# One decoder layer on one core: order of the last up-projection taps and of the residual row scaling

## The chip, the cores and the metric

The kernel runs on one core of one Trainium2 chip. The metric is the device time of an execution in microseconds; the time before is 735.07 us, the median of 3 runs (734.85 to 735.47). One further execution was profiled, and every duration below comes from it.

## The reference

One decoder layer with 512 tokens and a model width of 1024, in float32. Two causal attention branches on the same modulated input are gated, merged and projected; then a residual sum with a layer norm; then a gated MLP with a causal depthwise convolution of width 3 between the up-projection and the SiLU gate; then a second residual sum with a layer norm:

```python
x = _layer_norm(DEEPNORM_ALPHA * x + (1.0 + gt1) * attn_out, ln1_g, ln1_b)
u2 = x * (1.0 + sc2) + sh2
h = _causal_depthwise_conv(u2 @ w_up, conv_w, conv_b)
h_gate, h_val = jnp.split(h, 2, axis=-1)
ffn_out = (jax.nn.silu(h_gate) * h_val) @ w_down
x = _layer_norm(DEEPNORM_ALPHA * x + (1.0 + gt2) * ffn_out, ln2_g, ln2_b)
```

`w_up` is 1024 x 5632 and `w_down` 2816 x 1024. The change touches the stage that computes `h` and the start of the stage behind it.

## The kernel before, in words

**Products.** Every float32 operand is split into a high half (rounded to fp32r) and a low half (the rest), and each product is three matmuls: high x high, high x low, low x high (`mm3`, lines 152 to 154; `product`, lines 1148 to 1150). For weights, `split_proc` makes the halves `wh` on ACT (line 217) and `wl` on DVE (line 94).

**The up-projection** is a loop over 44 tiles n = 0 to 43, each of 128 columns (`for n in range(2 * FT)`). A tile is 24 matmuls over 512 tokens into one PSUM bank `ps`. ACT reads the bank with an Identity that applies the last tap and the bias (line 1201), DVE adds the two other taps (lines 1202 and 1203). Only then is the bank free again. After an odd tile ACT computes SiLU of the gate (line 1209) and DVE multiplies (line 1210). After every fourth tile `blocks` prepares the operands of the down-projection, and `early_products` does 18 of its matmuls ahead (line 1148 to 1150). From tile 7 on, six of the eight banks hold sums of the down-projection (`yz`), so the up-projection has two banks, and tile n+2 takes the bank of tile n.

**Behind the loop** `phase(Z, zi, ...)` multiplies pairs of down-projection weights (`zi`, split by `split_cols`) into two new banks, `Z`. These are the two banks of tiles 42 and 43.

**Residual rows.** `x1[i]` holds the normalized rows of the first sub-layer (tiles named `xn`, four row blocks of two halves). They need scale and bias of the layer norm, times alpha, before the second residual sum. `o_x1(i, e)` does that for a half: one multiplication (line 975) and one addition (line 976) on DVE. The first call also loads the four half rows `lnr` by broadcasts on SP (`ln_row`, line 913) and lets ACT scale them (lines 916 and 919). It is called at the even tiles 6 to 20.

**Loads.** `weights(i, ahead)` asks for the weights of item i and those some items ahead: up-projection weights (`in_wup`), parts of `w_down` (`in_wdp`), columns of the modulation matrix (`in_wa`), whose products are summed on DVE by `mod_sum` (line 240). All go through five buffers `raw` by SP's queue. Two parts of `w_down` are added during the transfer by an accumulating load from POOL (line 181).

**What sets the order.** SP's loads stand in program order. The instructions of the other engines are put in order by the framework's scheduler, engine by engine, by its own estimates; a wait is placed only where data or a buffer asks for it. `tc.issue_after(x)` is an edge for this scheduler: the instruction does not stand ahead of x.

Of the kernel before, what the change touches and what calls it, by code (L numbers as in the profile page):

```python
# [11 lines left out]
AF = mybir.ActivationFunctionType  # L12
ALU = mybir.AluOpType
# [9 lines left out]
FT = DFF // P  # L23
# [28 lines left out]
def layer_kernel(ctx: ExitStack, tc: tile.TileContext, out, xT, x, c8, wa0, wa1, bcol, w1, wct, wv, bf,  # L52
# [3 lines left out]
    V, S, G, PE = nc.vector, nc.scalar, nc.gpsimd, nc.tensor  # L56
# [14 lines left out]
    cnt, state = [0], {"load": 0, "proc": 0}  # L71

    def nm(s):
        cnt[0] += 1
        return f"{s}_{cnt[0]}"

    def bank():
        return pp.tile([P, 512], F32, name=nm("ps"), tag="ps")
# [5 lines left out]
    def const(shape, dt, s):  # L84
        return cons.tile(shape, dt, name=s, tag=s)
# [7 lines left out]
    def lo_of(o, i, hi):  # L93
        state["read"] = V.tensor_tensor(o, i, fl(hi), ALU.subtract)  # L94
        return state["read"]
# [33 lines left out]
    g = G.tensor_copy(crow[0:KT], c8s)  # L129
# [18 lines left out]
    def z(dt, s, shape=(P, 512)):  # L148
        return zp.tile(list(shape), dt, name=nm(s), tag="z", bufs=NZ)
# [7 lines left out]
    reads, held, pins, convs = [], [], {}, []  # L157
# [56 lines left out]
    def split_proc(r, cols=1024):  # L214
        h = stg.tile([P, 1024], F32R, name=nm("wh"), tag="wh", bufs=WBUFS)
        l = stg.tile([P, 1024], F32R, name=nm("wl"), tag="wl", bufs=WBUFS)
        state["hi"] = S.activation(h[:, 0:cols], r[:, 0:cols], AF.Copy)  # L217
        lo_of(l[:, 0:cols], r[:, 0:cols], h[:, 0:cols])
        return h, l
# [477 lines left out]

    def split_cols(cols):
        def f(r):
            return split_proc(r, cols)  # L700
        return f

    stream, sums = [], []
# [206 lines left out]
    def ln_row(n):  # L910
        t = [z(F32, "lnr") for _ in range(2)]
        for e in range(2):
            nc.sync.dma_start(t[e], lnrow[n : n + 1, e * 512 : (e + 1) * 512].broadcast_to([P, 512]))
        if n % 2 == 0:
            for e in range(2):
                S.activation(t[e], t[e], AF.Copy, scale=-0.5 * ALPHA)
        else:
            for e in range(2):
                S.activation(t[e], t[e], AF.Copy, scale=ALPHA)
        return t  # L920

    cw = const([P, 2 * FT, 4], F32, "cw")
    nc.sync.dma_start(cw, cwb)
    x1 = []
    lnr = []
# [46 lines left out]
    def o_x1(i, e):  # L972
        if not lnr:
            lnr.extend([ln_row(0), ln_row(1)])
        V.tensor_tensor(x1[i][e], x1[i][e], lnr[0][e], ALU.mult)
        V.tensor_tensor(x1[i][e], x1[i][e], lnr[1][e], ALU.add)

    def raw_proc(r):
        return r
# [57 lines left out]
    for n in range(2 * FT):  # L1037
# [7 lines left out]
        if n in (23, 27):  # L1045
            t = t13[(23, 27).index(n)][:, 0:512]
# [11 lines left out]
    zi, vi, xi, cli, wi = [], [], [], [], []  # L1058
# [112 lines left out]
    for n in range(2 * FT):  # L1171
        if n < NSPLIT:
            h, l = items[wui[n]][4]
            ps = bks[n]
            up_mm(ps, h, l, slice(256, 512))
        else:
            ps = bank()
            h, l = weights(wui[n], min(LOADS - 1, wui[min(n + 2, 2 * FT - 1)] - wui[n]))
            up_mm(ps, h, l, slice(0, 512))
            if n % 2 == 0 and 6 <= n < 22:  # L1180
                o_x1((n - 6) // 4, n // 2 % 2 == 0)
            if n >= 7 and n % 4 == 3:
                early_products((n - 7) // 4)
            if n in (10, 28):
                weights(wai[n], 0)
            if n in (10, 30):
                rows = gate_rows(1 + n // 30, G)
                next(rows)
            if n in (11, 32):
                next(rows)  # L1190
        if n == 24:
            for i in range(2):
                lnr2.append(lnp.tile([P, D], F32, name=f"ln2_{i}", tag=f"ln2_{i}"))
                nc.sync.dma_start(lnr2[i], lnrow[2 + i : 3 + i, :].broadcast_to([P, D]))
        if n == 28:
            S.activation(lnr2[0], lnr2[0], AF.Copy, scale=-0.5)
        if n in (30, 32):
            S.dma_start(out[(n - 30) * 64 : (n - 30) * 64 + P, :], lnr2[1])
        t = z(F32, "cv")
        hc.append(t)  # L1200
        S.activation(t, ps, AF.Identity, bias=cw[:, n, 3:4], scale=cw[:, n, 2:3])  # L1201
        V.scalar_tensor_tensor(t[:, 1:], ps[:, 0:511], cw[:, n, 1:2], t[:, 1:], ALU.mult, ALU.add)  # L1202
        convs.append(V.scalar_tensor_tensor(t[:, 2:], ps[:, 0:510], cw[:, n, 0:1], t[:, 2:], ALU.mult, ALU.add))  # L1203
        if n > 3:
            next(work, None)
        if n % 2 == 1:
            g, v = hc
            hc = []
            S.activation(g, g, AF.Silu)  # L1209
            V.tensor_tensor(g, g, v, ALU.mult)  # L1210
            hs.append(g)
            if n % 4 == 3:
                work = blocks(*hs)
                hs = []
                if n < 2 * FT - 1:
                    next(work)
# [9 lines left out]
    r = x1  # L1226
# [92 lines left out]
    lnr = lnr2  # L1319
# [13 lines left out]
    for n, k in enumerate(wi):  # L1333
        w = weights(k)
        for a, p in enumerate(range(2 * n, min(FP - LATE, 2 * n + 2))):
            t = ops[p][3]
# [10 lines left out]
    for i in range(2):  # L1347
        pieces = [(1, 0, 512)] if i == 0 else [(1, 0, 256), (1, 256, 512)]
        for n, (e, c0, c1) in enumerate(pieces):
            ps = bank()[:, 0 : c1 - c0] if i else W1[0]  # L1350
            for m in range(2 * n):
                PE.matmul(ps, idr, rest[:, m * 256 : m * 256 + 256], start=m == 0, stop=False)
            for q in range(LATE):
                t = ops[FP - LATE + q][3]
# [75 lines left out]
```

## Time and profile before

| | |
|---|---|
| median of 3 runs | 735.07 us (734.85 to 735.47) |
| the profiled execution | 734.44 us, its span 732.6 us |
| PE busy | 723.3 us, 99% of the span |
| DVE busy | 600.7 us, 82% |
| ACT busy | 391.6 us, 53% |
| POOL busy | 87.9 us, 12% |
| granted clock of PE | 0.998 |

PE is the matmul engine, PEld its weight loads, DVE, ACT and POOL the vector, scalar and general engines, SP the engine that issues loads; q1 is SP's DMA queue, q0 POOL's, q10 ACT's. In a row of the timeline stand start and duration in us, the engine, the line, the operation, out<-in by the program's names, and in brackets the idle time before it and what ended it. A row of waits reads: who waited, for whom, us in total, times, the longest. Durations of single instructions overlap a little at their ends, so the distance between two starts tells what an instruction costs its engine. A line can be a helper's, and then the tile names tell which call it is.

### The profile page before, as it was taken

What the parts mean: (1) busy time and instruction counts of PE and PEld (TensorE: products, weight loads), DVE (VectorE), ACT (ScalarE), POOL (GpSimd) and SP (SyncE); (2) the same over time, 40 slices, a digit from 0 to 9 for tenths busy, and PEclk for the clock granted to TensorE, in tenths of its full rate; (3) what the DMA queues carried; (4) which work ended last, traced back from release to release, by engine and by line L of the source; (5) the groups of instructions that cost most, each with busy time, mean ns of one, the idle gap of its engine ahead of it and who ended that gap; (6) DMA issues with size and microseconds to landing.
All of it is one profiled execution on the core that took longest, in us unless ns stands there. A gap on an engine that the chain in (4) does not pass through costs nothing.

```text
span 732.6 us, 9845 instructions
## 1 busy us (share of the span) xinstructions
PE 723.3 (99%) x3444; PEld 602.2 (82%) x3444; DVE 600.7 (82%) x1041; ACT 391.6 (53%) x684; POOL 87.9 (12%) x142
## 2 busy tenths in 40 slices
PE   8999999999999999999999999999999999999996
PEld 5878888888888888888889888888888888888885
DVE  7978799778898886873687999977887787679996
ACT  5576466686885754442056553454453444347550
POOL 1045224352010000000000001000011010000010
PEclk9999999999999999999999999999999999999999
DMA  9953535423332241632075677577799777656734
GB/s 357 404 207 126 174 116 198 148 88 115 118 116 103 71 171 59 221 130 86 1 259 146 209 248 245 166 247 229 206 339 254 211 239 208 200 161 226 223 86 95
DMA packets 45490, 131.96 MB, mean 180 GB/s; under 512 B 6168, under 2 KB 7200, under 8 KB 45440
## 3 DMA queue, kind: packets, MB, share of 16 engines
q1 hardware_dynamic: 38176, 112.61, 44.7%
q0 software_dynamic: 4224, 10.30, 7.0%
q10 hardware_dynamic: 3040, 8.42, 3.1%
q8 instruction: 27, 0.44, 0.2%
q14 instruction: 23, 0.19, 0.1%
HBM read 118.39 MB, written 12.85 MB: 179 GB/s over the span
## 4 chain that ended last, share of the span: by engine, by line
PE 97%; DMA 1%; DVE 1%; ACT 0%; issue 0%; DVEq 0%
PE ps L152 19%; PE ps L154 19%; PE ps L153 19%; PE ps L1148 5%; PE ps L1149 5%; PE ps L1150 5%; PE ps L369 5%; PE ps L613 3%; PE ps L595 2%; PE ps L521 2%; PE ps L523 2%; PE ps L522 2%; PE ps L939 2%; PE ps L940 2%; PE ps L941 2%; PE ps L547 1%
## 5 line engine op out<-in xcount | busy, mean ns | idle before, releaser
L217 ACT ACTIVATE wh<-raw 128x1024 fp32r<-128x1024 f32 (+1 forms) x105 | 109.1, 1041 | 106.2 <-PE ps L153 44.3
L94 DVE TENSOR_TENSOR wl<-raw,wh 128x1024 fp32r<-128x1024 f32 (+2 forms) x114 | 137.2, 1204 | 33.2 <-ACT wh L217 32.4
L152 PE MATMUL ps<-u2h,wh 128*128 128x512 f32 (+1 forms) x376 | 141.4, 376 | 0.0
L153 PE MATMUL ps<-u2l,wh 128*128 128x512 f32 (+1 forms) x376 | 141.2, 375 | 0.0
L154 PE MATMUL ps<-u2h,wl 128*128 128x512 f32 (+1 forms) x376 | 141.2, 375 | 0.0
L154 PEld LDWEIGHTS ps<-u2h,wl 128*128 128x128 f32 x376 | 70.8, 188 | 12.8
L152 PEld LDWEIGHTS ps<-u2h,wh 128*128 128x128 f32 x376 | 70.8, 188 | 12.8
L153 PEld LDWEIGHTS ps<-u2l,wh 128*128 128x128 f32 x376 | 70.8, 188 | 12.6
L152 PE MATMUL ps<-uh,wh 128*128 128x512 f32 x200 | 79.5, 398 | 0.0
L154 PE MATMUL ps<-uh,wl 128*128 128x512 f32 x200 | 78.3, 391 | 0.0
L153 PE MATMUL ps<-ul,wh 128*128 128x512 f32 x200 | 77.9, 390 | 0.0
L1201 ACT ACTIVATE cv<-ps,cw 128x512 f32<-128x512 f32 x44 | 34.0, 773 | 46.6 <-PE ps L154 40.2
L1202 DVE SCALAR_TENSOR_TENSOR cv<-ps,cw,cv 128x511 f32<-128x511 f32 x44 | 32.8, 744 | 22.6 <-ACT cv L1201 22.6
L154 PEld LDWEIGHTS ps<-uh,wl 128*128 128x128 f32 x200 | 37.5, 188 | 8.6 <-DVE wl L94 0.3
L153 PEld LDWEIGHTS ps<-ul,wh 128*128 128x128 f32 x200 | 37.6, 188 | 7.4
L152 PEld LDWEIGHTS ps<-uh,wh 128*128 128x128 f32 x200 | 37.5, 188 | 7.4
L240 DVE SCALAR_TENSOR_TENSOR raw<-raw,cbc 128x1024 f32<-128x1024 f32 x32 | 39.5, 1238 | 0.0
L575 POOL TENSOR_TENSOR pt<-pt,om 128x127 f32<-128x127 f32 (+3 forms) x32 | 38.6, 1218 | 1.4 <-DVE om L574 1.3
L181 POOL DMA_DIRECT2D raw<-in_wdp x10 | 8.8, 885 | 245.1 <-DMA raw<-in_wdp 229.2
L1203 DVE SCALAR_TENSOR_TENSOR cv<-ps,cw,cv 128x510 f32<-128x510 f32 x44 | 32.7, 743 | 0.4
L574 DVE TENSOR_TENSOR_SCAN om<-om,dg 128x127 f32<-128x127 f32 (+3 forms) x32 | 28.8, 960 | 3.8 <-ACT om L569 3.8
L1209 ACT ACTIVATE cv<-cv 128x512 f32<-128x512 f32 x22 | 13.9, 631 | 33.0 <-DVE cv L1203 33.0
(245 smaller groups left out, 1550.1 us busy)
## 6 DMA issues: line engine op xcount, KB each, us to landing
raw<-in_wup SPq DMA_DIRECT2D x44, 512.0 KB, 5.1
raw<-in_wa SPq DMA_DIRECT2D x32, 512.0 KB, 3.5
raw<-in_wct SPq DMA_DIRECT2D x25, 512.0 KB, 4.5
raw<-in_wdp SPq DMA_DIRECT2D x20, 512.0 KB, 5.2
wa<-in_wa SPq DMA_DIRECT2D x16, 512.0 KB, 8.7
raw<-in_wdp SPq DMA_DIRECT2D x22, 256.0 KB, 4.6
raw<-t SPq DMA_DIRECT2D x22, 256.0 KB, 4.1
raw<-in_wdp POOLq DMA_DIRECT2D x10, 512.0 KB, 7.3
```

Source lines behind the costliest of these rows:

```text
L94: state["read"] = V.tensor_tensor(o, i, fl(hi), ALU.subtract)
L152: PE.matmul(ps, wh, ah, start=first, stop=False)
L153: PE.matmul(ps, wh, al, start=False, stop=False)
L154: return PE.matmul(ps, wl, ah, start=False, stop=last)
L217: state["hi"] = S.activation(h[:, 0:cols], r[:, 0:cols], AF.Copy)
L240: state["read"] = V.scalar_tensor_tensor(wt[:, c], wt[:, c], 1.0, cbc[:, c] if by is None else by, ALU.mult, ALU.mult, accum_out=o)
L369: m = PE.matmul(grp[g], w, u, start=j == 0 and n == 0, stop=j == KT - 1 and n == 2)
L575: G.tensor_tensor(pt[b][:, s : e - 1], pt[b][:, s : e - 1], om[:, s + 1 : e], ALU.mult)
L1148: PE.matmul(ps, ah, bh, start=first, stop=False, skip_group_check=onto)
L1149: PE.matmul(ps, ah, bl, start=False, stop=False, skip_group_check=onto)
L1150: return PE.matmul(ps, al, bh, start=False, stop=last, skip_group_check=onto)
L1201: S.activation(t, ps, AF.Identity, bias=cw[:, n, 3:4], scale=cw[:, n, 2:3])
```

## The change

Line numbers of the changed kernel are 4 to 10 higher behind the first edit (the taps are lines 1206 to 1208 there, the scaling 980 and 981, SiLU of the last tile 1217).

- The split of Z's weights from the second pair on (`zi[2:]` is compared with the item number) is to stand behind SiLU of the last pair of tiles on ACT and behind the last tap on DVE, once that SiLU exists.
- That SiLU is to stand behind the Identity of tile 43.
- `o_x1` is called at tiles 8 to 22 instead of 6 to 20, in the same order of halves, and each call is to stand behind the last tap of the tile before.

```diff
     def split_cols(cols):
         def f(r):
-            return split_proc(r, cols)
+            with ExitStack() as order:
+                if "tap" in state and state["proc"] in zi[2:]:
+                    order.enter_context(tc.issue_after(state["tap"].ins))
+                    order.enter_context(tc.issue_after(convs[-1].ins))
+                return split_proc(r, cols)
         return f
...
     def o_x1(i, e):
         if not lnr:
             lnr.extend([ln_row(0), ln_row(1)])
-        V.tensor_tensor(x1[i][e], x1[i][e], lnr[0][e], ALU.mult)
-        V.tensor_tensor(x1[i][e], x1[i][e], lnr[1][e], ALU.add)
+        with tc.issue_after(convs[-1].ins):
+            V.tensor_tensor(x1[i][e], x1[i][e], lnr[0][e], ALU.mult)
+            V.tensor_tensor(x1[i][e], x1[i][e], lnr[1][e], ALU.add)
...
-            if n % 2 == 0 and 6 <= n < 22:
-                o_x1((n - 6) // 4, n // 2 % 2 == 0)
+            if n % 2 == 0 and 8 <= n < 24:
+                o_x1((n - 8) // 4, n // 2 % 2 == 1)
...
-        S.activation(t, ps, AF.Identity, bias=cw[:, n, 3:4], scale=cw[:, n, 2:3])
+        tap = S.activation(t, ps, AF.Identity, bias=cw[:, n, 3:4], scale=cw[:, n, 2:3])
...
-            S.activation(g, g, AF.Silu)
+            with ExitStack() as order:
+                if n == 2 * FT - 1:
+                    order.enter_context(tc.issue_after(tap.ins))
+                    state["tap"] = S.activation(g, g, AF.Silu)
+                else:
+                    S.activation(g, g, AF.Silu)
```

What the scheduler makes of it, at three places. First ACT at the end of the loop, before and now (`cv_6187` is tile 42, `cv_6243` tile 43, `wh_6316` the high half of Z's third item of weights, `wdh` parts of the last down-projection weights):

```order
L1201 ACTIVATE cv_6187<-ps_6151,cw 128x512
L1209 ACTIVATE cv_6187<-cv_6187 128x512
L217 ACTIVATE wh_6316<-raw_6265 128x1024
L1201 ACTIVATE cv_6243<-ps_6191,cw 128x512
L91 ACTIVATE wdh_6268<-raw_6157 128x512
```

```order
L1206 ACTIVATE cv_6187<-ps_6151,cw 128x512
L1206 ACTIVATE cv_6243<-ps_6191,cw 128x512
L1217 ACTIVATE cv_6187<-cv_6187 128x512
L91 ACTIVATE wdh_6268<-raw_6157 128x512
L217 ACTIVATE wh_6316<-raw_6265 128x1024
```

The split moved from ahead of tile 43's Identity to behind it and one more split. DVE there, before and now:

```order
L1203 SCALAR_TENSOR_TENSOR cv_6187<-ps_6151,cw,cv_6187 128x510
L94 TENSOR_TENSOR wl_6317<-raw_6265,wh_6316 128x1024
L1202 SCALAR_TENSOR_TENSOR cv_6243<-ps_6191,cw,cv_6243 128x511
L1203 SCALAR_TENSOR_TENSOR cv_6243<-ps_6191,cw,cv_6243 128x510
L94 TENSOR_TENSOR wdl_6269<-raw_6157,wdh_6268 128x512
```

```order
L1207 SCALAR_TENSOR_TENSOR cv_6243<-ps_6191,cw,cv_6243 128x511
L1208 SCALAR_TENSOR_TENSOR cv_6243<-ps_6191,cw,cv_6243 128x510
L94 TENSOR_TENSOR wdl_6269<-raw_6157,wdh_6268 128x512
L1220 TENSOR_TENSOR cv_6187<-cv_6187,cv_6243 128x512
L94 TENSOR_TENSOR wdl_6274<-raw_6192,wdh_6272 128x512
L94 TENSOR_TENSOR wl_6317<-raw_6265,wh_6316 128x1024
```

The low half `wl_6317` moved from ahead of tile 43's taps to behind them, a product and two half-wide splits. Second, SP's loads around tile 8, before and now (`raw_4307` before and `raw_4305` now are tile 10's weights):

```order
L174 DMA raw_4127<-in_wup 128x1024
L913 DMA lnr_4173<-in_lnrow 128x512
L913 DMA lnr_4174<-in_lnrow 128x512
L913 DMA lnr_4179<-in_lnrow 128x512
L913 DMA lnr_4180<-in_lnrow 128x512
L174 DMA raw_4192<-in_wa 128x1024
L174 DMA raw_4194<-in_wup 128x1024
L174 DMA raw_4261<-in_wdp 128x1024
L174 DMA raw_4264<-in_wdp 128x512
L174 DMA raw_4307<-in_wup 128x1024
```

```order
L174 DMA raw_4127<-in_wup 128x1024
L174 DMA raw_4178<-in_wa 128x1024
L174 DMA raw_4180<-in_wup 128x1024
L174 DMA raw_4247<-in_wdp 128x1024
L174 DMA raw_4250<-in_wdp 128x512
L917 DMA lnr_4280<-in_lnrow 128x512
L917 DMA lnr_4281<-in_lnrow 128x512
L917 DMA lnr_4286<-in_lnrow 128x512
L917 DMA lnr_4287<-in_lnrow 128x512
L174 DMA raw_4305<-in_wup 128x1024
```

The four loads of `lnr` moved behind four weight loads. Third, DVE from tile 8's first tap to tile 9's, before and now (`cv_4296` and `cv_4294` are tile 8, `cv_4350` and `cv_4348` tile 9; the rows of `raw` alone are sums of parts of `w_down`):

```order
L1202 SCALAR_TENSOR_TENSOR cv_4296<-ps_4260,cw,cv_4296 128x511
L94 TENSOR_TENSOR fo_4301<-cv_4058,fh_4300 128x256
L1203 SCALAR_TENSOR_TENSOR cv_4296<-ps_4260,cw,cv_4296 128x510
L94 TENSOR_TENSOR fo_4301<-cv_4187,fh_4300 128x256
L999 TENSOR_TENSOR raw_4309<-raw_4309 128x512
L94 TENSOR_TENSOR wdl_4319<-raw_4309,wdh_4317 128x512
L94 TENSOR_TENSOR wl_4379<-raw_4372,wh_4378 128x1024
L94 TENSOR_TENSOR wdl_4320<-raw_4309,wdh_4318 128x512
L975 TENSOR_TENSOR xn_3452<-xn_3452,lnr_4173 128x512
L646 SCALAR_TENSOR_TENSOR gcol<-modr,bcols 128x4
L1202 SCALAR_TENSOR_TENSOR cv_4350<-ps_4306,cw,cv_4350 128x511
```

```order
L94 TENSOR_TENSOR wl_4310<-raw_4305,wh_4309 128x1024
L1207 SCALAR_TENSOR_TENSOR cv_4294<-ps_4246,cw,cv_4294 128x511
...
L1003 TENSOR_TENSOR raw_4307<-raw_4307,raw_4247 128x512
L94 TENSOR_TENSOR wl_4377<-raw_4370,wh_4376 128x1024
L1004 TENSOR_TENSOR raw_4307<-raw_4307 128x512
L94 TENSOR_TENSOR wdl_4317<-raw_4307,wdh_4315 128x512
L240 SCALAR_TENSOR_TENSOR raw_4374,modr<-raw_4374,cbc 128x1024
L94 TENSOR_TENSOR wdl_4318<-raw_4307,wdh_4316 128x512
L94 TENSOR_TENSOR wl_4381<-raw_4372,wh_4380 128x1024
L1207 SCALAR_TENSOR_TENSOR cv_4348<-ps_4304,cw,cv_4348 128x511
```

The low half of tile 10's weights (`wl_4310`) now stands ahead of tile 8's first tap, and a mod sum (L240) and tile 12's split (`wl_4381`) ahead of tile 9's, where a multiplication of the row scaling and a small sum stood. The rows of PE are the same in number; around the early products a few of them change places, and one early product stands ahead of tile 11 now.

## The prediction

> **What bounds the kernel now.** I read the page first (busy shares, then the chain that ended last), then the waits of the matmul engine, then the stage of the up-projection in stretches of one period, and only then single instructions. The page:
>
> ```profile
> PE 723.3 (99%) x3444; PEld 602.2 (82%) x3444; DVE 600.7 (82%) x1041; ACT 391.6 (53%) x684; POOL 87.9 (12%) x142
> ...
> PE 97%; DMA 1%; DVE 1%; ACT 0%; issue 0%; DVEq 0%
> ```
>
> PE is busy for 723.3 of 732.6 us and holds 97% of the chain. 99% could still hide short waits, so here are all the waits of PE that the trace lists:
>
> ```profile
> PE ps L229 <- DVE warm L107: 1.2, 1, 1.2
> PE ps L229 <- DVE wa L240: 0.3, 1, 0.3
> PE ps L369 <- DVE uh L331: 0.3, 1, 0.3
> ```
>
> All three (L229 and L369) belong to the first stage, far ahead of the change. What is left of the 9.3 us without PE is the start and the tail after the last matmul. The periods of four up-projection tiles (columns: stretch, length, then busy time of PE, PEld, DVE, ACT, POOL):
>
> ```profile
> 401.93:427.77 25.84, 25.84 (x115) 21.40 (x114) 22.70 (x39) 14.93 (x26) 0.87 (x1) 1.00 0.67 216
> 427.77:453.61 25.84, 25.84 (x115) 21.40 (x114) 25.16 (x43) 13.06 (x22) 2.95 (x5) 1.00 0.79 252
> 453.61:479.45 25.84, 25.84 (x115) 21.40 (x114) 22.89 (x41) 10.98 (x19) 2.02 (x3) 1.00 0.64 191
> 479.45:505.29 25.84, 25.84 (x115) 21.40 (x114) 21.73 (x36) 11.87 (x20) 1.47 (x2) 1.00 0.74 227
> ```
>
> Every period lasts the same 25.84 us with PE busy through all of it at the full granted clock (the 1.00). DVE is nearly full in the second (25.16), where the row scaling sits, and PE does not notice. So neither edit can shorten these stretches: what a gain would be made of is a PE wait, and there must be one in reach.
>
> **Edit one, the taps of the last tile.** Busy time alone does not show it, the starts of the matmuls do:
>
> ```profile
> 662.37 0.39 PE L1148 MATMUL ps<-wh,hv 128*128 128x512 f32 x1
> 662.60 0.39 PE L1149 MATMUL ps<-wl,hv 128*128 128x512 f32 x1
> 663.10 0.47 PE L1148 MATMUL ps<-wh,hv 128*128 128x512 f32 x1
> ```
>
> The first two start 0.23 us apart, as matmuls of this form do elsewhere; the next gap is 0.50. The matmul at 663.10 is the first into the second bank of Z, and that bank is the last tile's, free only when both DVE taps have read it:
>
> ```profile
> 659.21 1.04 ACT L217 ACTIVATE wh<-raw 128x1024 fp32r<-128x1024 f32 x1
> 660.16 0.76 ACT L1201 ACTIVATE cv<-ps,cw 128x512 f32<-128x512 f32 x1
> ...
> 660.29 1.22 DVE L94 TENSOR_TENSOR wl<-raw,wh 128x1024 fp32r<-128x1024 f32 x1 [1.71 <-ACT wh L217]
> 661.43 0.74 DVE L1202 SCALAR_TENSOR_TENSOR cv<-ps,cw,cv 128x511 f32<-128x511 f32 x1
> 662.21 0.75 DVE L1203 SCALAR_TENSOR_TENSOR cv<-ps,cw,cv 128x510 f32<-128x510 f32 x1
> ...
> 666.36 0.39 PE L1149 MATMUL ps<-wl,hv 128*128 128x512 f32 x1
> ```
>
> The second tap ends at 662.96, and PE goes on 0.14 later. The split of the third pair of Z's weights stands ahead on both engines (ACT 659.21, DVE 660.29). The change puts it behind: the ACT tap can start at 659.21 instead of 660.16, the DVE taps at 660.29 or before instead of 661.43, and they end by 661.82. PE wants the bank at 662.60 + 0.23 = 662.83. The wait of 0.50 - 0.23 = **0.27 us** is gone. The price: the DVE half of that split now follows the two taps, one product and two half-splits. From a start at 660.29 that is 1.53 + 3 x 0.61 + 1.14, so it ends near 664.8. PE reads it at 666.36, or 666.1 without the wait: covered, with 1.3 us to spare.
>
> **Edit two, the row scaling.** Its instructions and loads, in the view of the tile lnr:
>
> ```profile
> L975 DVE TENSOR_TENSOR xn<-xn,lnr x8: 677/682/683, 421.6 to 459.0; 128x512 f32<-128x512 f32 x8
> L976 DVE TENSOR_TENSOR xn<-xn,lnr x8: 678/682/693, 422.9 to 459.7; 128x512 f32<-128x512 f32 x8
> L913 SPq DMA_DIRECT2D lnr<-in_lnrow x4: 376/400/432, 410.6 to 412.1; - x4
> ```
>
> The 16 operations (0.68 us each, about 11 us) stay 16. They ran from 421.6 to 459.7 and now run on to tile 22. Spreading them gains nothing, since PE never waited for DVE there. A period receives four of them: 4 x 0.61 = 2.4 us on top of 21.73 in the period that had none makes 24.2 of 25.84. At tiles 10, 14, 18 and 22 they stand ahead of and between the taps and delay these by at most 1.2 us. That the bank bears, for example at tile 10:
>
> ```profile
> 448.53 0.74 DVE L1203 SCALAR_TENSOR_TENSOR cv<-ps,cw,cv 128x510 f32<-128x510 f32 x1
> ...
> 453.61 0.39 PE L152 MATMUL ps<-u2h,wh 128*128 128x512 f32 x1
> ```
>
> Tile 10's taps end at 449.27, tile 12 takes the bank at 453.61: 4.3 us to spare. All this costs nothing.
>
> What is not free is that **the four loads of lnr move** behind four weight loads on SP, straight ahead of tile 10's weights. DMA traffic from 405 to 440 us, and the instructions that I use:
>
> ```profile
> q1 hardware_dynamic: 2160, 6.55, 56.3%
> q0 software_dynamic: 144, 0.52, 8.6%
> ...
> 423.00 0.38 SPq L174 DMA_DIRECT2D raw<-in_wup  x1
> ...
> 424.98 0.87 POOL L181 DMA_DIRECT2D raw<-in_wdp  x1 [29.72 <-DMA raw<-in_wdp]
> ...
> 425.37 1.21 DVE L240 SCALAR_TENSOR_TENSOR raw<-raw,cbc 128x1024 f32<-128x1024 f32 x1
> ...
> 426.51 0.74 DVE L1203 SCALAR_TENSOR_TENSOR cv<-ps,cw,cv 128x510 f32<-128x510 f32 x1
> ...
> 428.48 1.06 ACT L217 ACTIVATE wh<-raw 128x1024 fp32r<-128x1024 f32 x1 [0.58 <-DMA raw<-in_wup]
> ...
> 434.56 0.74 DVE L1202 SCALAR_TENSOR_TENSOR cv<-ps,cw,cv 128x511 f32<-128x511 f32 x1
> 435.22 0.41 DVE L94 TENSOR_TENSOR fo<-cv,fh 128x256 fp32r<-128x256 f32 x1
> 435.55 0.74 DVE L1203 SCALAR_TENSOR_TENSOR cv<-ps,cw,cv 128x510 f32<-128x510 f32 x1
> 436.21 0.42 DVE L94 TENSOR_TENSOR fo<-cv,fh 128x256 fp32r<-128x256 f32 x1
> 436.54 0.68 DVE L999 TENSOR_TENSOR raw<-raw 128x512 f32<-128x512 f32 x1
> 437.15 0.68 DVE L94 TENSOR_TENSOR wdl<-raw,wdh 128x512 fp32r<-128x512 f32 x1
> 437.75 1.22 DVE L94 TENSOR_TENSOR wl<-raw,wh 128x1024 fp32r<-128x1024 f32 x1
> 438.88 0.69 DVE L94 TENSOR_TENSOR wdl<-raw,wdh 128x512 fp32r<-128x512 f32 x1
> ...
> 438.42 0.39 PE L154 MATMUL ps<-u2h,wl 128*128 128x512 f32 x1
> ...
> 444.09 0.39 PE L152 MATMUL ps<-u2h,wh 128*128 128x512 f32 x1
> ```
>
> SP's queue (q1) moved 6.55 MB in 56.3% of 35 us, 0.33 MB per us of engine time. Tile 10's weights were asked for at 423.00 and landed about 428.5, when ACT split them. Call their new landing X. Four lnr loads are 1.05 MB, 3.2 us, now ahead of them: X = 431.7 at best. POOL's accumulating load (0.52 MB, 8.6% of 35 us = 3.0 us) shares the engines; it was beside this load before too, but now it meets the lnr loads as well. If all of it counts, X = 434.7. Below 431.7 nothing speaks for it, as the bytes ahead are certain. The nearest row, the old landing beside the same accumulate, lies by the low end; a third to a half of the accumulate is new, so I take **X = 432.9**.
>
> What hangs on X: in the new order ACT's split of tile 10 comes after the lnr scaling and ahead of tile 8's tap, DVE's split likewise, and the tap waits behind them. ACT 1.06 and DVE 1.14 put tile 8's first tap at X + 2.2. From there to the end of tile 9's second tap DVE now has: two taps 0.66 each and two half-splits 0.33 each, four 512-wide operations 0.61, two 1024-wide splits 1.13, the mod sum 1.14 (drawn forward from behind tile 9, with a split of tile 12), tile 9's taps 0.66 and 0.74 with 0.34 between. All are start-to-start distances of the rows above (the mod sum's is 425.37 to 426.51, the 0.34 is taken like the 0.33). Sum 9.56 us. The tap ends at X + 11.8, and PE can go on at X + 11.9. Tile 11 takes this bank at 444.09, plus 0.23 for one early product that now comes first: 444.32. So PE waits X - 432.4, if positive: 0 at X = 431.7, **0.5 us** at 432.9, 2.3 us at 434.7. Where X is early, ACT's order sets a floor: tile 12's split takes a buffer that tile 9's last matmul (438.42 + 0.39) gives up, and half of the down weights follows (0.6); with 1.06 for the split that is 440.5, and DVE's last five operations (0.61, 1.13, 0.66, 0.34, 0.74) end near 444.0, 0.3 us in time. Tile 8's own bank, wanted when tile 10 starts (438.42 + 0.23), holds out to X near 434.6. Once the loads have caught up, tile 12 on has its old spare.
>
> **Sum.** 0 for the spreading, -0.27 for Z's bank, +0.5 at tile 11: +0.2. Span 732.6 to 732.8. The profiled execution took 734.44 (1.8 us around its span), the median of the runs is 735.07; I put the difference on the median: **735.3 us**. About 0.2% (1.5 us) is what a measurement of this kernel tells from no change, so the forecast is no change.
>
> **Rivals.**
> 1. *No wait at tile 11.* X stays under 432.4 since the lnr loads fill holes of the queue (it is busy only 56.3% of those 35 us). The 0.27 is kept: 734.8. Against it: at 423 the queue holds loads back to back. 33%.
> 2. *Slower: the lnr loads push tile 10's weights past the taps.* Place: tile 8 and 9's taps, tile 11's bank. Price X - 432.4; it decides from X = 434.2, where the net passes 1.5 us. With the whole accumulate in the way X = 434.7 and the time 735.07 + 2.3 - 0.27 = 737.1. For it: the row of q0, 3.0 us. Against: part of that was already in the old landing. 10%. The Trainium skill's page "DMA: Bandwidth & Descriptors" (section "Queues, rings and completion order") speaks for this case: each DMA engine takes turns between queues, packet by packet. By that rule the accumulate's packets would all be paid by the loads beside it, and the sum would be that of this rival; the old landing agrees with a part at most.
> 3. *Faster, because DVE is relieved.* If the packed period (25.16 of 25.84) hid PE waits of some tenths per tile, 735.07 less 2, say 733. Against it: that period is as long as those without scaling. 2%.
> 4. *Edit one does nothing*: the bank's wait passes to the split that was moved back. Then 735.07 + 0.5 = 735.6. Against it: the 1.3 us to spare. 5%.
>
> **How the numbers follow.** My forecast holds 50%, the rivals 33, 10, 2 and 5. Forecast, rivals 1 and 4 are all within 0.2%: 88%, of which I give 1 to slower, for a wait that I have not seen: same 0.87, slower 0.11, faster 0.02. Range: rival 1 less 0.4 for the spread of medians (the runs differ by 0.6) gives 734.4; above, X = 434.2 gives 735.07 + 1.8 - 0.27 = 736.6. It leaves out the worse half of rival 2 and rival 3.
>
> **What would show it.** Right: matmuls at the second bank of Z start 0.23 apart; the four periods still 25.84 but for one near 444 that is some tenths longer, with the gap ahead of tile 11; tile 10's split on ACT at 432 to 434, idle before it put down to its load. Wrong: a period from 427 to 453 that is unchanged (rival 1) or over 2 us longer (rival 2); shorter periods anywhere (rival 3); a gap at 663 still there (rival 4); or a wait of PE at a tile from 12 to 24, which I have costed at nothing.

## The result, and where the time went

The changed kernel takes 735.90 us (median of 22 runs, 734.64 to 736.90), the kernel before 734.86 us (22 runs, 734.17 to 735.88): ratio 1.0015, 95% interval 1.0009 to 1.0020. That is 1.05 us more. It lies within the 0.2% that the prediction called no change, 0.6 us above the forecast of 735.3. But the interval leaves out 1: the change costs a little, and the loss is real.

The page of the changed kernel looks like the one of before (first row: busy us of each engine; then the chain that ended last):

```profile
PE 722.7 (99%) x3444; PEld 602.4 (82%) x3444; DVE 601.2 (82%) x1041; ACT 392.3 (54%) x684; POOL 88.0 (12%) x142
...
PE 97%; DMA 1%; DVE 1%; ACT 0%; issue 0%; DVEq 0%
```

Its profiled execution has a span of 732.9 us, 734.64 us as timed: the fastest of its 22 runs. In it the periods are as they were (the first three of the four; columns as in the prediction):

```profile
401.93:427.77 25.84, 25.84 (x116) 21.40 (x115) 23.31 (x40) 14.27 (x24) 2.89 (x5) 1.00 0.58 188
427.77:453.61 25.84, 25.84 (x116) 21.40 (x115) 22.71 (x37) 14.27 (x24) 1.47 (x2) 1.00 0.93 286
453.61:479.45 25.84, 25.84 (x116) 21.40 (x115) 20.95 (x37) 11.11 (x19) 1.43 (x2) 1.00 0.60 180
```

PE is busy through all of them, and through the fourth. So this one execution shows no loss in the up-projection, although the kernel loses 1 us in the median. A second profile of the same kernel, taken in the third set of runs (span 734.5, 736.30 us as timed), shows where it goes. The same stretch, and the matmuls at the start of tile 11:

```profile
427.77:453.61 25.84, 24.97 (x111) 20.35 (x110) 22.12 (x37) 14.75 (x25) 2.92 (x5) 1.00 0.91 272
```

```profile
444.65 0.39 PE L1153 MATMUL ps<-wdh,hv 128*128 128x512 f32 x1
445.90 0.50 PE L152 MATMUL ps<-u2h,wh 128*128 128x512 f32 x1 [0.87 <-DVE cv L1208]
```

0.87 us of PE are missing from the stretch, and the matmul at 445.90 starts 1.25 us after the one ahead of it in place of 0.23. It is tile 11's first, and waits for the second tap of tile 9 (L1208 is the line of the second taps here). That is the place and the chain of the prediction. From before's profile to this one the span grows by 1.9 us: 1.2 at tile 11 (the wait, and matmuls right behind it that start late), 0.5 in the tail, 0.3 less at Z, and 0.6 that is lost ahead of the up-projection, which the change does not touch.

**Two executions, one chain.** The first fence is the profiled execution of 732.9 us, the second the one of 734.5 (timelines of ACT, DVE and PE; L217 is the ACT half of a weight split, L94 on `wl` the DVE half):

```profile
431.19 1.06 ACT L217 ACTIVATE wh<-raw 128x1024 fp32r<-128x1024 f32 x1 [1.48 <-DMA raw<-in_wup]
438.72 1.06 ACT L217 ACTIVATE wh<-raw 128x1024 fp32r<-128x1024 f32 x1 [0.63 <-PE ps L153]
443.31 0.74 DVE L1208 SCALAR_TENSOR_TENSOR cv<-ps,cw,cv 128x510 f32<-128x510 f32 x1
444.19 0.39 PE L1153 MATMUL ps<-wdh,hv 128*128 128x512 f32 x1
444.41 0.39 PE L152 MATMUL ps<-u2h,wh 128*128 128x512 f32 x1
```

```profile
433.34 1.06 ACT L217 ACTIVATE wh<-raw 128x1024 fp32r<-128x1024 f32 x1 [2.55 <-DMA raw<-in_wup]
437.79 1.06 ACT L217 ACTIVATE wh<-raw 128x1024 fp32r<-128x1024 f32 x1 [2.12 <-DMA raw<-in_wup]
438.88 1.23 DVE L94 TENSOR_TENSOR wl<-raw,wh 128x1024 fp32r<-128x1024 f32 x1 [0.64 <-ACT wh L217]
442.98 1.22 DVE L94 TENSOR_TENSOR wl<-raw,wh 128x1024 fp32r<-128x1024 f32 x1
445.11 0.74 DVE L1208 SCALAR_TENSOR_TENSOR cv<-ps,cw,cv 128x510 f32<-128x510 f32 x1
```

Tile 10's split, idle before it for its load as foretold, starts at 431.19 in the one and at 433.34 in the other. In the first the tap ends at 443.31 + 0.74 = 444.05, on the floor of 444.0 that ACT's order sets (the split at 438.72 waits for PE), and PE needs the bank at 444.41. In the second the tap ends at 445.85. The row loads moved, too: they are asked for at 421.0 to 422.4 in place of 410.6 to 412.1, and the scaling now runs on to 525.5 (view of the tile lnr):

```profile
L981 DVE TENSOR_TENSOR xn<-xn,lnr x8: 680/684/696, 430.7 to 525.5; 128x512 f32<-128x512 f32 x8
L917 SPq DMA_DIRECT2D lnr<-in_lnrow x4: 422/426/441, 421.0 to 422.4; - x4
```

**Z's bank.** Here the change does what it says (combined timeline of the changed kernel):

```profile
659.27 0.78 ACT L1206 ACTIVATE cv<-ps,cw 128x512 f32<-128x512 f32 x1 [3.75 <-PE ps L154]
660.87 0.75 DVE L1208 SCALAR_TENSOR_TENSOR cv<-ps,cw,cv 128x510 f32<-128x510 f32 x1
662.30 0.39 PE L1155 MATMUL ps<-wh,hv 128*128 128x512 f32 x1
662.53 0.40 PE L1153 MATMUL ps<-wh,hv 128*128 128x512 f32 x1
662.77 0.39 PE L1154 MATMUL ps<-wl,hv 128*128 128x512 f32 x1
663.34 1.22 DVE L94 TENSOR_TENSOR wl<-raw,wh 128x1024 fp32r<-128x1024 f32 x1
```

The second tap ends at 661.62 (662.96 before), the matmuls start 0.23 apart, and the split that went behind ends at 664.56 with no wait after it.

**The tail.** No step of the prediction has it. From the start of the last matmul to the end of the span it is 8.0 us in the changed kernel (724.88 to 732.9) and 7.5 in the one before (725.12 to 732.6). The section on the hardware comes back to this half microsecond.

### The profile page after: what moved, and what is told of

Read it like the earlier page. It is cut to its first block, busy times and chain, and to the rows that moved or that the text cites. A ratio compares the mean times of both kernels' runs of the same rounds, so it can differ in the third digit from the quotient of the medians.

```text
span 732.9 us, 9836 instructions
## 1 busy us (share of the span) xinstructions
PE 722.7 (99%) x3444; PEld 602.4 (82%) x3444; DVE 601.2 (82%) x1041; ACT 392.3 (54%) x684; POOL 88.0 (12%) x142
## 4 chain that ended last, share of the span: by engine, by line
PE 97%; DMA 1%; DVE 1%; ACT 0%; issue 0%; DVEq 0%
PE ps L152 19%; PE ps L154 19%; PE ps L153 19%; PE ps L1153 5%; PE ps L1155 5%; PE ps L1154 5%; PE ps L369 5%; PE ps L613 3%; PE ps L595 2%; PE ps L521 2%; PE ps L523 2%; PE ps L522 2%; PE ps L944 2%; PE ps L945 2%; PE ps L943 2%; PE ps L547 1%
## 5 line engine op out<-in xcount | busy, mean ns | idle before, releaser
L94 DVE TENSOR_TENSOR wl<-raw,wh 128x1024 fp32r<-128x1024 f32 (+2 forms) x114 | 137.1, 1204 | 34.2 <-ACT wh L217 33.0
L217 ACT ACTIVATE wh<-raw 128x1024 fp32r<-128x1024 f32 (+1 forms) x105 | 109.1, 1041 | 103.2 <-PE ps L153 48.6
L240 DVE SCALAR_TENSOR_TENSOR raw<-raw,cbc 128x1024 f32<-128x1024 f32 x32 | 39.7, 1242 | 0.0
L575 POOL TENSOR_TENSOR pt<-pt,om 128x127 f32<-128x127 f32 (+3 forms) x32 | 38.6, 1217 | 1.4 <-DVE om L574 1.3
L1208 DVE SCALAR_TENSOR_TENSOR cv<-ps,cw,cv 128x510 f32<-128x510 f32 x44 | 32.8, 744 | 0.4
L1219 ACT ACTIVATE cv<-cv 128x512 f32<-128x512 f32 x21 | 13.3, 631 | 34.6 <-DVE cv L1208 30.6
```

The lines of the kernel that those rows point to most:

```text
L240: state["read"] = V.scalar_tensor_tensor(wt[:, c], wt[:, c], 1.0, cbc[:, c] if by is None else by, ALU.mult, ALU.mult, accum_out=o)
L575: G.tensor_tensor(pt[b][:, s : e - 1], pt[b][:, s : e - 1], om[:, s + 1 : e], ALU.mult)
```

## The experiments

All times are medians; the three sets ran on three chips, and each has its own runs of the kernel before beside it (734.87, 734.60 and 734.59 us). The ratios and their intervals are estimated from all runs and can differ by 0.0003 from the quotient of two medians. "Early rows" below is the changed kernel with its four lnr loads where they were before.

| kernel | median us (runs) | ratio to before, 95% | PE gap beyond 0.23 at tile 11, profiled | tail, profiled |
|---|---|---|---|---|
| changed | 735.90 (22) | 1.0015 [1.0009, 1.0020] | 0 | 8.0 |
| changed, again | 735.88 (11) | 1.0015 [1.0006, 1.0024] | 1.02 | 8.0 |
| edit one alone | 734.48 (11) | 0.9997 [0.9988, 1.0005] | 0 | 7.5 |
| edit two alone | 736.21 (11) | 1.0015 [1.0006, 1.0024] | 0.88 | 8.0 |
| early rows | 734.38 (11) | 0.9994 [0.9985, 1.0003] | 0 | 7.5 |
| not behind the convolutions | 735.96 (11) | 1.0014 [1.0005, 1.0022] | 1.04 (the early product ahead of it) and 0.43 | 7.5 |
| no accumulating load | 734.83 (11) | 1.0006 [0.9998, 1.0015] | 0 | 8.1 |
| rows on ACT's queue | 743.41 (4) | 1.0119 [1.0105, 1.0133] | 6.4 at tile 10 | 7.9 |
| old tiles, behind | 734.45 (11) | 0.9995 [0.9986, 1.0004] | 0 | 7.5 |
| early rows, again | 734.27 (11) | 0.9997 [0.9988, 1.0006] | 0 | 7.5 |
| tile 12's split behind | 734.74 (11) | 1.0004 [0.9995, 1.0013] | 0 | 8.0 |
| half the row bytes | 734.88 (11) | 1.0003 [0.9994, 1.0012] | 0 | 8.0 |
| early rows, third | 734.44 (11) | 0.9997 [0.9989, 1.0006] | 0 | 7.5 |

### Which edit, and where: four kernels

The theories. A: the late row loads make tile 10's weights late, and PE waits at tile 11. B: the last scalings, now at tiles 20 and 22, reorder DVE at tiles 23 to 26, and PE waits at tile 26; for B spoke that the spare of tile 26's weight split shrank from 1.67 us to 0.34 in the changed kernel's profile. C: edit one itself costs.

Edit one alone, from the changed kernel:

```diff
-        with tc.issue_after(convs[-1].ins):
-            V.tensor_tensor(x1[i][e], x1[i][e], lnr[0][e], ALU.mult)
-            V.tensor_tensor(x1[i][e], x1[i][e], lnr[1][e], ALU.add)
+        V.tensor_tensor(x1[i][e], x1[i][e], lnr[0][e], ALU.mult)
+        V.tensor_tensor(x1[i][e], x1[i][e], lnr[1][e], ALU.add)
...
-            if n % 2 == 0 and 8 <= n < 24:
-                o_x1((n - 8) // 4, n // 2 % 2 == 1)
+            if n % 2 == 0 and 6 <= n < 22:
+                o_x1((n - 6) // 4, n // 2 % 2 == 0)
```

> Edit one alone: the last tile's taps ahead of the weight splits, the row scaling as in the kernel before. All theories but one: 0.27 us under the kernel before (ratio 0.9996), the matmul gap of 0.50 us at Z's second bank gone. Theory C (edit one itself costs what was measured): about 1.0 us over it (ratio 1.0015).

Edit two alone is the kernel before with the same lines the other way round.

> Edit two alone: the row scaling at tiles 8 to 22 behind the convolutions, Z's bank as before (gap of 0.50 us stays). Theory A (late row loads: tile 10's weights late, PE waits for tile 9's bank at tile 11 in most executions) and theory B (the last scalings push a weight split so far back that tile 26 waits for it in most executions): 1.3 us over the kernel before (ratio 1.0018), the changed kernel's 1.0 and edit one's 0.27. Theory C: no difference from before.

Early rows:

```diff
+            if n == 6:
+                lnr.extend([ln_row(0), ln_row(1)])
             if n % 2 == 0 and 8 <= n < 24:
                 o_x1((n - 8) // 4, n // 2 % 2 == 1)
```

> The changed kernel, with the four row loads asked for at tile 6 as before, so that they stand ahead of tile 8's weights again; the scaling stays at tiles 8 to 22. Theory A: the loss is gone, 0.27 us under before (ratio 0.9996), and the second tap of tile 9 ends 2 us ahead of its need at tile 11. Theory B: the order on DVE and ACT at tiles 23 to 26 is the changed kernel's, so the loss stays, 1.0 us over before (ratio 1.0015), with the gap at tile 26.

Not behind the convolutions:

```diff
-        with tc.issue_after(convs[-1].ins):
-            V.tensor_tensor(x1[i][e], x1[i][e], lnr[0][e], ALU.mult)
-            V.tensor_tensor(x1[i][e], x1[i][e], lnr[1][e], ALU.add)
+        V.tensor_tensor(x1[i][e], x1[i][e], lnr[0][e], ALU.mult)
+        V.tensor_tensor(x1[i][e], x1[i][e], lnr[1][e], ALU.add)
```

> The changed kernel without the rule that the scaling is issued behind the last convolution: the same tiles 8 to 22 ask for it, the row loads stand late as in the changed kernel, but the scaling is drawn forward to tiles 8 to 12 and the order at tiles 23 to 26 is that of before. Theory A: 1.0 us over before (ratio 1.0015), gap at tile 11. Theory B: 0.27 us under before (ratio 0.9996), no gap from tile 20 on.

Measured: 0.39 us under before, 1.34 over, 0.49 under, 1.09 over. C falls with the first two. B falls with the last two: early rows keep the order at tiles 23 to 26 and lose nothing, and the kernel with late rows and the old order there loses as much as the changed one. (Its loss is made up otherwise: the tail is that of before, the waits around tile 11 are longer, since there DVE does eight operations of the row scaling ahead of tile 10's split in place of two.) A holds, and its gap is in the profile of edit two alone:

```profile
433.73 1.06 ACT L217 ACTIVATE wh<-raw 128x1024 fp32r<-128x1024 f32 x1 [3.40 <-DMA raw<-in_wup]
444.77 0.75 DVE L1204 SCALAR_TENSOR_TENSOR cv<-ps,cw,cv 128x510 f32<-128x510 f32 x1
444.46 0.39 PE L1149 MATMUL ps<-wdh,hv 128*128 128x512 f32 x1
445.57 0.50 PE L152 MATMUL ps<-u2h,wh 128*128 128x512 f32 x1 [0.72 <-DVE cv L1204]
```

With early rows the split stands 5.3 us earlier and the tap 2.7 (third set's profile); the tap ends 1.45 us ahead of its need, where 2 were expected:

```profile
428.42 1.06 ACT L217 ACTIVATE wh<-raw 128x1024 fp32r<-128x1024 f32 x1 [0.65 <-DMA raw<-in_wup]
442.12 0.74 DVE L1210 SCALAR_TENSOR_TENSOR cv<-ps,cw,cv 128x510 f32<-128x510 f32 x1
444.31 0.39 PE L152 MATMUL ps<-u2h,wh 128*128 128x512 f32 x1
```

One thing in the profile of edit one alone was not expected. It shows no gap at Z or tile 11, but at tile 14 a matmul that starts 0.99 us after the one ahead of it, 0.76 more than the usual 0.23, and it was the slowest of its 11 runs (736.13):

```profile
465.39 0.39 PE L154 MATMUL ps<-u2h,wl 128*128 128x512 f32 x1
466.38 0.47 PE L152 MATMUL ps<-u2h,wh 128*128 128x512 f32 x1 [0.61 <-DVE cv L1207]
```

With the scaling packed into tiles 6 to 12 as before, an execution in which DVE runs late does make PE wait for tile 12's taps. One execution shows it; how often it happens is open.

### What makes tile 10's weights late

A1: the rows (1.05 MB) push the weights back into POOL's accumulating load, which then costs them most. A2: the rows' bytes alone are enough. The third kernel asks whether the place in SP's queue matters or the late request; the fourth, whether tiles 8 to 22 are worth anything beside tiles 6 to 20.

No accumulating load (the one that POOL issues near 425 us is left out, so one sum of down-projection weights is missing; the order on ACT and DVE is the changed kernel's):

```diff
-        items[-1].append(wdp[p][:, 512:1536])
+        if p != 1:
+            items[-1].append(wdp[p][:, 512:1536])
```

> The changed kernel without one transfer: POOL's accumulating load of 0.52 MB (raw from wdp, the one that starts near 429 us) is left out, so the output lacks one sum of down-projection weights; every other instruction stands where it stood, the row loads late. Theory A1 (the rows only push tile 10's weights into the accumulating load, whose packets then alternate with theirs): tile 10's split starts by 430.5, no gap at tile 11, the time falls to that with early rows, ratio 0.9994. Theory A2 (the 1.05 MB of the rows ahead are enough): tile 10's split still at 433 or later, the gap at tile 11 stays, ratio 1.0015.

Rows on ACT's queue:

```diff
-            nc.sync.dma_start(t[e], lnrow[n : n + 1, e * 512 : (e + 1) * 512].broadcast_to([P, 512]))
+            nc.scalar.dma_start(t[e], lnrow[n : n + 1, e * 512 : (e + 1) * 512].broadcast_to([P, 512]))
```

> The changed kernel with the four row loads issued by ACT in place of SP, just as late. If their place ahead of tile 10's weights in SP's queue is what costs (theory A, either form): tile 10's split starts within 1 us of the 428.5 of before, no gap at tile 11, ratio 0.9994. If late rows cost by their bytes wherever they are queued, or by holding up the first scaling on DVE: ratio 1.001 or more, with a gap between tiles 9 and 12.

Old tiles, behind the convolutions:

```diff
-            if n % 2 == 0 and 8 <= n < 24:
-                o_x1((n - 8) // 4, n // 2 % 2 == 1)
+            if n % 2 == 0 and 6 <= n < 22:
+                o_x1((n - 6) // 4, n // 2 % 2 == 0)
```

> The changed kernel with the scaling asked for at tiles 6 to 20 as before, but still behind the convolutions: rows early, Z's bank freed earlier. Theory A: no gap at tile 11, ratio 0.9994 as with early rows at tiles 8 to 22. If the shift to tiles 8 to 22 had a gain of its own beside the late rows: slower than the run with early rows by that gain, at most 0.3 us (ratio 0.9998).

Early rows, again:

> The changed kernel with early rows once more, as the candidate for a better version: theory A expects 0.27 to 0.5 us under before (ratio 0.9994 to 0.9996), and an interval over both sets of runs that leaves out 1. If the first set was luck: ratio 1.000.

Without the accumulating load no gap is left, and the time is 0.23 us over the runs of before beside it, where the changed kernel is 1.05 and 1.29 over. So A2 falls, by the time: the profile alone would not do, since its start of tile 10's split lies within the spread of the kernels that have this load (431.19 to 433.92). Two numbers were missed. Tile 10's split starts at 432.51 and not by 430.5, just early enough; and the time stays 0.56 us above early rows in the same set, which is the tail (8.1 against 7.5).

```profile
432.51 1.06 ACT L217 ACTIVATE wh<-raw 128x1024 fp32r<-128x1024 f32 x1 [1.45 <-DMA raw<-in_wup]
443.55 0.73 DVE L1209 SCALAR_TENSOR_TENSOR cv<-ps,cw,cv 128x510 f32<-128x510 f32 x1
444.47 0.39 PE L152 MATMUL ps<-u2h,wh 128*128 128x512 f32 x1
```

How the accumulating load costs can be read from the DMA view of the changed kernel's second profile (q1 is SP's queue, q0 POOL's; packets, MB, share of the 16 engines). First 428 to 430.5 us, then 431 to 434:

```profile
q1 hardware_dynamic: 341, 0.91, 100.6%
...
q0 software_dynamic: 104, 0.43, 70.8%
q1 hardware_dynamic: 110, 0.39, 35.3%
```

Alone, q1 moves 0.91 MB in 2.5 us, 0.36 MB per us. Beside the accumulate both move about as many packets, 110 and 104, but those of q0 take two thirds of the engines' time, and q1 is down to 0.39 MB in 3 us, 0.13 MB per us. Late by the rows, tile 10's weights and the ones behind them run into this; before, they had landed by 428.48, when 0.13 MB of the accumulate had moved (423 to 428.1 us of the kernel before):

```profile
q1 hardware_dynamic: 344, 0.95, 51.4%
q0 software_dynamic: 32, 0.13, 18.1%
```

The Trainium skill's page "DMA: Bandwidth & Descriptors", section "Queues, rings and completion order", says that a DMA engine goes round its queues packet by packet; the 110 against 104 packets agree.

The cost falls on two loads, and more on the second. From its request to its split, tile 10's load takes 8.1 us without the accumulate (424.40 to 432.51) and 8.2 to 9.8 in the five profiles that have it and all the rows late on SP's queue: 0.1 to 1.7 us more. Tile 11's load, the next weights of the up-projection, takes 9.4 us from request to landing without it (425.67 to 435.05) and 11.7 to 12.2 with it: 2.4 to 2.8 us more.

Rows on ACT's queue were far slower than either view of A. Tile 10's split did start early, at 427.63, but ACT issued the rows only then, and they landed from 436.9 on, beside the accumulate:

```profile
427.64 2.06 ACTq L917 DMA_DIRECT2D lnr<-in_lnrow  x4
436.96 0.63 ACT L920 ACTIVATE lnr<-lnr 128x512 f32<-128x512 f32 x1 [8.26 <-DMA lnr<-in_lnrow]
438.56 0.39 PE L154 MATMUL ps<-u2h,wl 128*128 128x512 f32 x1
445.21 0.77 PE L152 MATMUL ps<-u2h,wh 128*128 128x512 f32 x1 [6.26 <-DVE cv L1208]
```

The scaling of the rows stands ahead of tile 8's taps on ACT and DVE, so these waited for the rows, and PE waited 6.4 us for tile 8's bank. The order on the engines assumes rows in time; that they are late is paid by whatever is queued behind them. The wait was not the whole price. Behind it PE ran at half its clock (row of 445 to 450 us, columns as above: the granted clock is the 0.50):

```profile
445.00:450.00 5.00, 4.79 (x11) 3.80 (x12) 4.66 (x11) 4.29 (x9) 0.66 (x1) 0.50 0.81 256
```

Until 451 us the matmuls start 0.43 us apart in place of 0.23, and that adds 2.8 us to the 6.4. Behind the 1.0 us wait of the changed kernel's second profile the clock stays at 1.00 in the same stretch.

Old tiles with early rows: 734.45 against 734.27, so the shift to tiles 8 to 22 has no gain that 11 runs can tell.

### The chain to tile 9's tap

The changed kernel a second time, for its profile (shown above):

> The changed kernel once more, for a second profile beside the same runs of before. Theory A (PE waits for tile 9's bank at tile 11, in most executions by 1 to 2 us): 1.0 us over before (ratio 1.0015), and the profiled execution has a gap at 444 to 445 us whose size is its own lateness; if this one has no gap, its time is near that of the run with early rows.

Tile 12's split behind: one condition where the weights are split; on DVE it puts one instruction, `wl` of tile 12 (the 1.22 us at 442.98 above), behind tile 9's taps. On ACT only a Silu (L1219) moved, behind the two instructions that followed it.

```diff
-    reads, held, pins, convs = [], [], {}, []
+    reads, held, pins, convs, wup12 = [], [], {}, [], {}
...
+            with ExitStack() as order:
+                if len(items) > 9 and it[0] is wup12.get(0):
+                    order.enter_context(tc.issue_after(convs[9].ins))
-            it[4] = it[1](it[3])
+                it[4] = it[1](it[3])
...
+        if n == 12:
+            wup12[0] = items[-1][0]
```

> The changed kernel with one instruction elsewhere: the DVE half of tile 12's weight split (1.13 us), which the change put ahead of tile 9's taps, goes behind them again; rows late, tile 10's weights late. Theory A: the DVE chain to tile 9's second tap is 1.13 us shorter, so the wait at tile 11 shrinks by up to that in each execution; of a mean wait of 1.5 us some 0.4 stay: ratio 1.0001. If the loss is not at tile 9's taps: ratio 1.0015 as without.

Half the row bytes:

```diff
-            nc.sync.dma_start(t[e], lnrow[n : n + 1, e * 512 : (e + 1) * 512].broadcast_to([P, 512]))
+            nc.sync.dma_start(t[e][:, 0:256], lnrow[n : n + 1, e * 512 : e * 512 + 256].broadcast_to([P, 256]))
...
-                S.activation(t[e], t[e], AF.Copy, scale=ALPHA)
+                S.activation(t[e][:, 256:512], t[e][:, 0:256], AF.Copy, scale=ALPHA)
```

> The changed kernel with half the bytes in the late row loads: each loads 128 by 256 and ACT's scaling copies it to the other half, so the scaled rows are wrong; tile 12's split falls back behind tile 9's taps on both engines by itself. 0.52 MB ahead of tile 10's weights in place of 1.05: their landing 1.6 us earlier by the queue's rate, and more if they then escape the accumulating load. Theory A: no wait at tile 11, ratio 0.9995. If bytes in the queue don't matter (only the late request does): the same as with tile 12's split behind the taps and full rows.

Early rows, third:

> The changed kernel with early rows a third time: 0.3 to 0.5 us under before (ratio 0.9994 to 0.9996); over all three sets of runs the mean ratio stays below 1. If there is no gain: 1.000.

Moving one DVE instruction of 1.13 us out of the chain took 735.88 - 734.74 = 1.14 us off the time, although tile 10's split is as late as ever (432.81):

```profile
432.81 1.06 ACT L220 ACTIVATE wh<-raw 128x1024 fp32r<-128x1024 f32 x1 [2.76 <-DMA raw<-in_wup]
442.84 0.74 DVE L1213 SCALAR_TENSOR_TENSOR cv<-ps,cw,cv 128x510 f32<-128x510 f32 x1
444.31 0.39 PE L152 MATMUL ps<-u2h,wh 128*128 128x512 f32 x1
```

The tap ends at 443.58, 0.73 ahead of its need; with the 1.13 us still ahead of it, it would have been 0.4 late. This is the test that shows that the loss sits in this chain. Half the bytes took 1.00 us off; there tile 10's split starts at 429.51. But in that kernel tile 12's split went behind tile 9's taps as well, and other DVE instructions changed places, so its time does not tell the bytes from the order; only the earlier landing speaks for the bytes. Both kernels stay 0.3 to 0.44 us above early rows, about the 0.5 of the tail that they share with the changed kernel.

The version with early rows is 1.44 us faster than the changed kernel in the set that has both; in the two others it is 0.49 and 0.33 us under before, where the changed kernel is 1.05 over. Against the kernel before, its three ratios lie at 0.9994 to 0.9997, each interval with 1 in it: faster by some 0.3 us is likely, and not shown.

## Why the prediction was right, and where it was not

The forecast was a change of +0.2 us, and +1.05 was measured. The place, the chain and the sign were right; of the size only a quarter was, and that the time still lies near the forecast is partly owed to the width of what was called no change. The intervals here are 0.05% to 0.1% to either side, so 0.2% was a coarser measure than the runs allow.

- **PE bound, nothing to win in the periods.** Right for what the profile of before showed; one execution of edit one alone had a wait for DVE at tile 14, so "PE never waited for DVE there" holds for most executions, not all.
- **Z's bank, -0.27.** Right. From the last up-projection matmul to the last matmul it is 66.38 us in the profile of before, and 66.03 to 66.09 in the twelve profiles of kernels with edit one: a gain of 0.3. Edit two alone, without edit one, has 66.18, so the wait differs between the two profiles that have it, and the gain may be smaller in other executions. In the medians a gain of 0.3 us is too small to show (edit one alone: ratio 0.9997, 0.9988 to 1.0005). The split that went behind ended at 664.56 (forecast 664.8) and made nobody wait. Rival 4 falls.
- **Tile 10's weights at X = 432.9, between 431.7 and 434.7.** The lower bound was too high: the quickest profiled execution had 431.19. Half of its lead over the slowest comes from SP, which asked for the loads 1.4 us earlier there; the other half was gained in the queue. The four others with late rows, all their bytes and the accumulating load, all on SP's queue, had 432.81 to 433.92. So X is not a number but a spread of 2.7 us over executions. Its middle was forecast well: the mean of the five is 433.0.
- **X + 11.8 for the tap, and a wait of X - 432.4.** Right to a tenth where nothing else in the chain waits, when X and PE's own start are taken from each profile; of the four below, one has a wait to test it, one is short of it and one lies on the floor. PE's start is that of tile 8's first matmul, 427.77 before:

| profile | X | tile 8 starts | X + 11.8 | tap ended | wait by the formula | measured |
|---|---|---|---|---|---|---|
| changed | 431.19 | 427.87 | floor 444.0 | 444.05 | 0 | 0 |
| changed, again | 433.34 | 428.33 | 445.14 | 445.85 | 0.38 | 1.02 |
| edit two alone | 433.73 | 428.14 | 445.53 | 445.52 | 0.96 | 0.88 |
| no accumulating load | 432.51 | 427.92 | 444.31 | 444.28 | 0 | 0 |

  The one miss has its cause in the rows above: tile 11's weights were late as well (437.79), and DVE stood idle 0.64 us for them inside the chain. 0.38 + 0.64 = 1.02.
- **The sum's term for tile 11, +0.5.** This is the term that was mis-sized: 0.8 to 1.1 in the median. (The kernel without that one DVE instruction in the chain, and with the same tail, takes 1.14 us less; the sum at the end of this section leaves 0.8 to 1.1.) Tile 10's weights are not much of the reason: I had counted 1.2 of the accumulating load's 3.0 us for them, and 0.1 to 1.7 were measured. The prediction put the loads behind them at nothing. Tile 11's weights pay 2.4 to 2.8 us of that load, and their split stands in the same chain on DVE. And a wait has no negative side: an X that is early by a microsecond gains nothing, one that is late by as much is paid, so the mean wait is more than the wait at the mean X. How much of the missing 0.3 to 0.6 us is owed to each is open.
- **Rival 1, no wait at tile 11.** Its sign, an unchanged period from 427 to 453, is in the first profile, and there it holds: X was 431.19. The median and the second profile show that it is the exception. Rival 2's price of +2.3 asks for X = 434.7, and no profile came so far (433.92 at most). Rival 3 falls: no period is shorter.
- **The tail.** The prediction took it as unchanged, without a reason. It cost 0.5.
- **The base.** I put the sum on the median of three runs, 735.07; over 22 runs it is 734.86. So the forecast of the time misses by 0.6 us and that of the change by 0.8: the difference is luck.

Together: -0.3 at Z, +0.5 in the tail, and so some +0.8 to +1.1 at tile 11 make the measured 1.05 over 734.86 (1.29 in the third set).

## What to carry to other kernels

A rule that moves work to later can also move the first use of its inputs, and with it their loads: look at what the loads are now queued ahead of, and what else is on the engines at that time. Where a load was hidden with little to spare, one profile is one draw from a spread: here the profiled execution was the fastest of 22 and had none of the loss, and a second profile showed it at once. A chain in order on one engine can be priced closely from start-to-start rows, as long as nothing inside it waits, and moving one instruction out of it is the cheapest test of whether it bounds.

## What the runs showed of the hardware that was not expected

**SP stands still for 0.34 us at fixed places, 128 instructions apart, and between the last writes that costs time.** The last three writes of the output as SP issued them (timeline of SP: the row of all three, then from the second on), first the changed kernel, then early rows (third set):

```profile
728.62 1.59 SPq L1262 DMA_DIRECT2D out<-xn  x3
729.37 0.84 SPq L1262 DMA_DIRECT2D out<-xn  x2
```

```profile
728.75 1.30 SPq L1264 DMA_DIRECT2D out<-xn  x3
729.19 0.86 SPq L1264 DMA_DIRECT2D out<-xn  x2
```

The second write is issued 0.75 us after the first in the changed kernel and 0.44 with early rows; the span ends 4.25 and 3.79 us after the first.

Number SP's instructions in the order of the trace, waits included. In all 14 profiles SP pauses for 0.34 to 0.35 us between its 207th and 208th instruction; the same pause comes between the 335th and 336th and between the 463rd and 464th, each time 128 further on. (In one profile, not behind the convolutions, a longer wait for data covers the last two.) Where the third pause falls in the tail depends on how many instructions came before. The changed kernel has 482 in all, and its 463rd is the first of the last three writes, so the second is late. With early rows there are 484, the 463rd is an earlier write, and SP has nothing to do for 2.4 us behind it anyway. The profiles fall into groups by this: 483 to 486 instructions (485 in the kernel before) and a tail of 7.5 us; 481 or 482 and 8.0 to 8.1. Rows on ACT's queue has 479: there the pause falls between the second and the third write, which are 0.79 us apart, and the tail is 7.9.

Behind the third pause the queue q14, which the page calls "instruction", moves a packet of 8 KB, in every profile 1.0 to 1.4 us after the 463rd instruction. In the changed kernel it is among the transfers after 728.5 us, with early rows among those between 723 and 728.5 (DMA view):

```profile
q14 instruction: 1, 0.01, 0.3%
```

```profile
q14 instruction: 1, 0.01, 0.9%
```

In the changed kernel it starts at 730.38, when SP has issued all three writes (the last by 730.21). So SP does not wait for the packet to land. That it asks for its next instructions in the pause is inferred and not shown. The later second write explains 0.3 of the 0.5 us; the rest passes after the third write, and its cause is open. A kernel that differs from the changed one by a few idle instructions on SP alone was not tried.

The Trainium skill's page "Runtime: NRT & Kernel Launch", section "Instruction fetch mechanics", says that each engine's sequencer fetches its instructions in blocks while it runs on, and that the cost of a block is mostly hidden. Here the pause is hidden where SP idles, and shows where it falls between the last writes of the kernel.
